# A third K panel combined in ten of the eleven up-projection groups, with raw blocks and scratch rows in four fixed tiles and the filters in two buffers

## The chip, the cores and the metric

The kernel runs on one core of one Trainium2 chip. The metric is the device time of one execution in microseconds, as the median of several runs. Before the change it is 1975.53 us (three runs, 1974.62 to 1976.78).

## The reference

One layer of a hybrid streaming encoder runs over two request groups that share the weights: a prompt of 256 rows and eight samples of 16 rows, 384 rows in all. The change lies in the last part, the feed-forward network. DM is 2048 and D_FF is 5632, all in float32:

```
h2 = rmsnorm(x, norm_ffn_g)
up = h2 @ w_up                              # (rows, 2048) @ (2048, 11264)
g_half = up[..., :D_FF]
u_half = up[..., D_FF:]
ext_f = jnp.concatenate([ffn_buf.astype(g_half.dtype), g_half], axis=1)
gc = causal_dwconv(ext_f, ffn_dw_w, ffn_dw_b)   # 3 taps along the rows, a filter per column
x = x + (jax.nn.silu(gc) * u_half) @ w_down     # (rows, 5632) @ (5632, 2048)
```

The output also holds the last two rows of `ext_f` for the prompt and each sample.

## The kernel before

**Operands.** Every weight comes as blocks of 512 KB, two slabs of 128 rows by 512 columns, by one DMA of the SP queue each (`fetch`). A block of float32 is split into a high half, which ScalarE casts to fp32r (line 166, "hi"), and a low half, which VectorE subtracts (line 167, "lo"). A product of 128 rows is then three matmuls: with hi, with lo, and the row operand's own low half with hi (lines 1169 to 1171 in the up groups, 313 to 315 elsewhere). One block with the products made from it is a **step**; the steps of a group are counted from 0. The high and the low half stand in pairs of tiles, three pairs in the feed-forward part (`depth`, two and SPARE), so a step's split can run up to three steps ahead of TensorE.

**Up groups.** The up projection runs in eleven groups g = 0 to 10. A group makes 512 columns of the gate half (g) and the same 512 of the other half (u). Its 2048 rows of K are four panels of 512, each with two blocks for g and two for u. A plain panel multiplies the three row tiles (two of the prompt, one of the samples) with all four blocks: 4 steps of 18 matmuls, 72. A **combined** panel (`MIXED`, here panels 0 and 1) treats the prompt's two row halves, the two K halves and the two column sets as a 2 by 2 product of blocks, and makes it with seven products in place of eight, from sums of blocks on both sides. Its steps are, in the words of `steps`, b22, t3, t1, b11, t2 in the first part of the group and b21, t4 in the second, with 12, 12, 6, 12, 6, 12 and 6 matmuls, 66. t1 to t4 are sums of blocks, made by VectorE: t3 is b22 + b12 in a tile of its own (line 208), t1 is b12 + b11 in place (line 213), and t2 and t4 add b11 and b21 to the running sum (line 217). A combined panel takes seven splits and four sums, a plain one four splits. The row side's sums ("xm") are made once, while the output projection runs (`combined`); plain panels read the rows' own halves ("xg"). A group before has 22 steps and 276 matmuls.

**The order.** TensorE's order is written out by hand: the steps of a group one after the other. Other engines are ordered by a scheduler with priorities: a split is put 150 places ahead (SPLIT_AHEAD), an eviction in this part 250 (FFN_AHEAD). Each engine then works strictly in its order, and an instruction that waits holds back all behind it. `after(units, fn)` puts side work at a later tick; there is a tick per three products, that is per nine matmuls. The groups follow each other by

```
FFN_PLAN = [("up", 0)]
for n in range(0, 8, 2):
    FFN_PLAN += [("up", n + 1), ("up", n + 2), ("down", (n, n + 1))]
FFN_PLAN += [("up", 9), ("up", 10), ("down", (8, 9, 10))]
```

so groups 0, 1 and 2 come in a row, then a stretch of the down projection for the two oldest groups, and so on. A **first** group (3, 5, 7, 9) follows a down stretch, a **second** one (2, 4, 6, 8, 10) follows another up group. The last down stretch takes three groups.

**Raw blocks.** Blocks are loaded into a rotation of tiles: three called "raw", S0 and S1 from the start of this part, and S2 and S3. The down projection's partial sums ("part") use S2 and S3 too, so after a down stretch a group first loads eight blocks (ROOM) into the other five; a group that follows an up group may use all seven from its start. A load into a block begins when the low half (or the sum) that read it last is done.

**Behind a group.** Eight products gather in PSUM. The evictions (`p7`, `p1`, `q6` and so on, lines 1212 to 1247) build the rows of u and g with the help of two scratch rows e0 and e1, which are the third row of the tile "sums". The rows are then turned so that columns lie on partitions (`turned`: VectorE transposes blocks of 32 at line 328, GpSimd's DMA queue moves them through DRAM and back). Then comes the filter, four parts m = 0 to 3 of 128 columns: `fill` copies a part into a row with room for the two frames ahead (ScalarE's line 1118, then four small copies on GpSimd, lines 1121 to 1125), `taps` makes three taps and SiLU (one tap on ScalarE, line 1139, two on VectorE, line 1141), and `product` multiplies with u and splits the result for the down projection. The filter of group g runs within the next stretch: `fill` for all four parts at tick 9, the taps of part m at 10 + 2m, its product at 13 + 2m. Group 10 has 7 and a pace of 1. The rows stand in four tiles "extf" and four "gc".

**Down projection.** TensorE makes 128 by 512 products of the groups' rows; ScalarE copies them to "part", and GpSimd's queue adds them to y in DRAM. In the last stretch y is loaded back and the sum goes to the output.

Of the kernel before, what the change touches and what calls it, by code (L numbers as in the profile page):

```python
# [34 lines left out]
MIXED = (0, 1)  # L35
ROOM, SPARE = 8, 1
# [6 lines left out]
def hybrid_step(  # L43
# [90 lines left out]
    slots, wide = ["raw", "raw", "raw", "S0", "S1", "S2", "S3"], [False]  # L134

    def fetch(srcs, by_row=False, more=0):
        ok = ["raw"] + (["S0", "S1", "S2", "S3"][:2 + more] if wide[0] else [])
        slot = next(s for s in slots if s in ok)
        slots.remove(slot)
        slots.append(slot)  # L140
        if slot != "raw":
            raw = p_sg.tile([P, 2, 512], F32, tag=slot, name="raw")
        else:
            raw = wp.tile([P, 2, 512], F32, tag="raw", bufs=3, name="raw")
# [9 lines left out]
    depth = [2]  # L154
# [26 lines left out]
    PLAIN = [q for q in range(4) if q not in MIXED]  # L181
# [10 lines left out]
    def planned_mixed(w, c1, c2, first, room):  # L192
        held, count = {}, [0]

        def load(rows):
            count[0] += 1
            return fetch([rows], more=2 if count[0] > room else 0)[0]
# [25 lines left out]
        for what, q in steps(first):  # L223
# [27 lines left out]
    for what, g in FFN_PLAN:  # L251
        if what == "up":
            planned_mixed(w_up, 512 * g, DFF + 512 * g, g == 0, ROOM if g % 2 or g == 0 else 0)
# [36 lines left out]
    def gemm(jobs, sides=()):  # L290
        for js in jobs:
# [4 lines left out]
            for j, k in [(j, k + i) for k in range(0, js[0]["nk"], 2) for j in js for i in range(2)]:  # L296
# [19 lines left out]
                if sp:  # L316
                    with tc.high_priority(offset=FFN_AHEAD if wide[0] else EVAC_AHEAD):
# [634 lines left out]
    def pw_job(g):  # L952
# [8 lines left out]
        def done():  # L961
# [10 lines left out]
            for m in range(4):  # L972
# [13 lines left out]
    xg = {q: p_x2.tile([P, 2, 4, NT], F32R, name=f"xg{q}") for q in range(4) if q not in MIXED}  # L986
    xm = {q: [(gp.tile([P, 10, 2, P], F32R, tag="G4", name="xm") if (q, i) == (MIXED[-1], 0) else
               p_x2.tile([P, 10, 2, P], F32R, name=f"xm{q}{i}"))[:] for i in range(2)] for q in MIXED}
# [20 lines left out]
    def combined(n, d):  # L1009
# [27 lines left out]
        after(5, add_up)  # L1037
        after(6, halves)
        after(7, plain)

    def wo_job(n):
# [11 lines left out]
        def done():  # L1053
            d = box[0].moved()

            def parts(m):
# [3 lines left out]
                if n not in MIXED:  # L1060
# [5 lines left out]
            if n in MIXED:  # L1066
# [27 lines left out]
    extf = [p_f.tile([P, 24, 18], F32, name=f"extf{m}")[:] for m in range(4)]  # L1094
    for m in range(4):
# [4 lines left out]
    wide[0] = True  # L1100
# [6 lines left out]
    def up_g_done(g, rows, gd):  # L1107
        def done():
# [5 lines left out]
            def fill():  # L1114
                for m in range(4):
                    c = 4 * g + m
                    e = extf[m]
                    nc.scalar.copy(e[:, :, 2:18].rearrange("p (a h) x -> p a h x", h=2),
                                   gd[:, :, m, :].rearrange("p a (h x) -> p a h x", h=2))
                    e5 = e.rearrange("p (i t h) x -> p i t h x", t=NTT, h=2)  # L1120
# [218 lines left out]
```

## Time and profile before

| | before |
|---|---|
| median of three runs | 1975.53 us |
| the profiled execution | 1974.45 us |
| its span | 1972.7 us |
| clock granted to TensorE | 1.00 |
| weight loads of w_up, w_in, w_down at 512 KB | 176, 96, 88 |
| turns through DRAM: out, in (median to landing) | 120 of 192 KB (4.5 us), 30 of 768 KB (5.8 us) |
| partial sums added to y in DRAM | 16 of 768 KB (6.8 us) |

The profiled execution is one run, recorded by the hardware; its own time is 1974.45 us, of which the records span 1972.7. The feed-forward part starts at 912.6 us: groups 0 to 2 last 193.2 us, each down stretch of two groups 65.3, each pair of up groups 125.6 to 126.3, and the last down stretch 97.9.

How to read the lines that follow. The head of the page gives for each engine its busy time, its share of the span and its number of instructions (PE is TensorE's matmuls, PEld its weight loads, DVE is VectorE, ACT ScalarE, POOL GpSimd, SP SyncE, which issues the weight loads). The view by stretches gives each engine's busy time in a window. The time line has a row for each instruction: start, duration, engine, line, operation, what is written and read, the shape, and in brackets how long the engine stood idle before it and what ended that. Matmuls overlap in the pipe, so their price is the distance between two starts. The view of waits gives an engine's idle time by what it was waiting for: us, times, longest. The chain is the work that ended last in a window, each row released by the one above it. A GEMM part that waits for nothing is full at TensorE's own pace; each wait of TensorE is lost time.

### The profile page before, as it was taken

The numbers are of one execution on the slowest core, as the hardware profiler recorded it, in microseconds if no ns is written. First come the engines' busy times: TensorE is split into PE (matmuls) and PEld (weight loads), VectorE is DVE, ScalarE is ACT, GpSimd is POOL, SyncE is SP. The second block draws the span as 40 slices with busy tenths as digits, with TensorE's granted clock in tenths as the row PEclk, the third lists the DMA queues.
The fourth block names the chain that finished last, engine by engine and source line by source line (L and its number), as shares of the span: only waits on it lengthen the run. The fifth ranks groups of instructions, "written<-read, shape, count | busy, mean of one in ns | idle before, by whom it ended". The sixth has DMA issues, their size and how long they took to land. (4 is left out here: it accounts for less than half of the span.)

```text
span 1972.7 us, 24795 instructions
## 1 busy us (share of the span) xinstructions
PE 1958.7 (99%) x9254; PEld 1648.7 (84%) x9254; DVE 1265.2 (64%) x1681; ACT 887.9 (45%) x1297; POOL 254.8 (13%) x527
## 2 busy tenths in 40 slices
PE   9999999999999999999999999999999999999999
PEld 9999878888888888887887888888888888888887
DVE  4478889747465447466787647855775577557853
ACT  5433353555324423345465444553454445444541
POOL 1001121100000002111122200220022012201210
PEclk9999999999999999999999999999999999999999
DMA  6565776665344438767665576567556755666653
GB/s 185 155 173 156 229 240 201 204 183 158 113 129 128 128 128 273 234 207 228 196 186 187 172 202 182 158 188 200 162 187 180 198 178 174 194 173 193 202 188 110
DMA packets 194899, 358.20 MB, mean 182 GB/s; under 512 B 16386, under 2 KB 66557, under 8 KB 194771
## 3 DMA queue, kind: packets, MB, share of 16 engines
q1 hardware_dynamic: 172779, 272.78, 44.5%
q0 software_dynamic: 21680, 83.70, 15.4%
q8 instruction: 72, 1.18, 0.2%
q14 instruction: 48, 0.39, 0.1%
q10 hardware_dynamic: 320, 0.14, 0.0%
HBM read 301.78 MB, written 55.24 MB: 181 GB/s over the span
## 5 line engine op out<-in xcount | busy, mean ns | idle before, releaser
L167 DVE TENSOR_TENSOR lo<-raw,hi 128x1024 fp32r<-128x1024 f32 (+2 forms) x481 | 578.4, 1203 | 519.3 <-ACT hi L166 517.6
L166 ACT CAST hi<-raw 128x1024 fp32r<-128x1024 f32 (+2 forms) x481 | 497.8, 1036 | 798.1 <-PE acc L315 468.4
L313 PE MATMUL acc<-hi,hT 128*128 128x512 f32 (+1 forms) x704 | 270.4, 384 | 0.1
L314 PE MATMUL acc<-lo,hT 128*128 128x512 f32 (+1 forms) x704 | 265.7, 377 | 1.3 <-DVE lo L167 1.3
L315 PE MATMUL acc<-hi,hT 128*128 128x512 f32 (+1 forms) x704 | 265.6, 377 | 0.0
L313 PE MATMUL acc<-hi,act 128*128 128x512 f32 x484 | 188.3, 389 | 0.0
L314 PE MATMUL acc<-lo,act 128*128 128x512 f32 x484 | 188.3, 389 | 0.0
L315 PE MATMUL acc<-hi,act 128*128 128x512 f32 x484 | 188.3, 389 | 0.0
L1170 PE MATMUL acc<-lo,xg 128*128 128x512 f32 x440 | 171.7, 390 | 2.8 <-DVE lo L167 2.8
L1171 PE MATMUL acc<-hi,xg 128*128 128x512 f32 x440 | 171.4, 389 | 0.4 <-DVE xg L1063 0.4
L1169 PE MATMUL acc<-hi,xg 128*128 128x512 f32 x440 | 171.2, 389 | 0.0
L314 PEld LDWEIGHTS acc<-lo,hT 128*128 128x128 f32 x704 | 132.3, 188 | 24.5 <-DVE lo L167 3.2
L579 DVE SCALAR_TENSOR_TENSOR ut<-ext,cw,ut 128x384 f32<-128x384 f32 x240 | 149.2, 622 | 5.5
L313 PEld LDWEIGHTS acc<-hi,hT 128*128 128x128 f32 x704 | 132.2, 188 | 24.0 <-issue 1.8
L315 PEld LDWEIGHTS acc<-hi,hT 128*128 128x128 f32 x704 | 132.2, 188 | 22.7
L333 POOL DMA_DIRECT2D turn<-block x124 | 69.0, 563 | 429.3 <-DVE block L328 422.5
L1170 PE MATMUL acc<-lo,xm 128*128 128x512 f32 x308 | 120.0, 389 | 0.2 <-DVE lo L167 0.2
L1169 PE MATMUL acc<-hi,xm 128*128 128x512 f32 x308 | 119.9, 389 | 0.0
L1171 PE MATMUL acc<-hi,xm 128*128 128x512 f32 x308 | 119.8, 389 | 0.0
L314 PEld LDWEIGHTS acc<-lo,act 128*128 128x128 f32 x484 | 90.9, 188 | 18.9
L313 PEld LDWEIGHTS acc<-hi,act 128*128 128x128 f32 x484 | 90.9, 188 | 18.8
L315 PEld LDWEIGHTS acc<-hi,act 128*128 128x128 f32 x484 | 90.9, 188 | 18.8
(349 smaller groups left out, 3404.6 us busy)
## 6 DMA issues: line engine op xcount, KB each, us to landing
raw<-in_w_up_dram SPq DMA_DIRECT2D x176, 512.0 KB
raw<-in_w_in_dram SPq DMA_DIRECT2D x96, 512.0 KB
raw<-in_w_down_dram SPq DMA_DIRECT2D x88, 512.0 KB
turn<-block POOLq DMA_DIRECT2D x120, 192.0 KB, 4.5
block<-turn POOLq DMA_DIRECT2D x30, 768.0 KB, 5.8
raw<-in_w_in_dram SPq DMA_DIRECT2D x64, 256.0 KB
raw<-in_w_out_dram SPq DMA_DIRECT2D x32, 512.0 KB
y_rows<-part POOLq DMA_DIRECT2D x16, 768.0 KB, 6.8
```

The source lines that it names most:

```text
L166: nc.scalar.copy(hi[:, k, :o], raw[:, k, :o])
L167: tt(lo[:, k, :o], raw[:, k, :o], f(hi[:, k, :o]), op=ALU.subtract)
L313: mm(o, ah[:, s], hi[:, kk, :n], start=st, stop=False)
L314: mm(o, ah[:, s], lo[:, kk, :n], start=False, stop=False)
L315: mm(o, al[:, s], hi[:, kk, :n], start=False, stop=sp)
L333: nc.gpsimd.dma_start(d[:, :, i, :].rearrange("j r n -> r j n"), src[32 * i:32 * i + 32, :].rearrange("r (j n) -> r j n", j=4))
L579: stt(o, v, wc, o, op0=ALU.mult, op1=ALU.add)
L1169: mm(o, ah, hi[:, kk, :], start=st, stop=False)
L1170: mm(o, ah, lo[:, kk, :], start=False, stop=False)
L1171: mm(o, al, hi[:, kk, :], start=False, stop=last[b] == (i, n))
```

## The change

Panel 2 (`BOTH`) joins the combined panels in groups 1 to 10 (`TRIPLE`, `mixed_of`); group 0 keeps two. Such a group has 25 steps and 270 matmuls, in this order: b22, t3, t1, a plain u block, b11, t2 of panel 0; b22, t3, t1, b11, t2 of panel 1; the same five of panel 2; a plain u block, a plain g block; b21 and t4 of panels 0, 1 and 2; a plain g block. Panel 2's running sum takes the third row of "sums".

To make room, four tiles "rest" of three rows are allotted once. Their first two rows are raw blocks, so that the rotation has seven blocks at all times (no ROOM); the third rows of two of them are e0 and e1, of the other two the filter's "gc". "part" stands in two scratch blocks that the turns use too. There are two "extf" and two "gc" in place of four: `fill` goes part by part, at tick 8 + 2m, the taps at 9 + 2m, the product at 11 + 2m (group 10: 7 + m, 8 + m, 9 + m). The row side's sums for panel 2 are made at ticks 10 and 11 of the output projection; its plain forms are read from xg2, so "xm" has five entries there. In the last down stretch y takes the four "rest" tiles, and its third and fourth quarters are loaded 14 ticks later than the first two.

```diff
-MIXED = (0, 1)
-ROOM, SPARE = 8, 1
+BOTH = 2
+TRIPLE = (1, 2, 3, 4, 5, 6, 7, 8, 9, 10)
+SPARE = 1
+def mixed_of(g):
+    return (0, 1, BOTH) if g in TRIPLE else (0, 1)
...
-    slots, wide = ["raw", "raw", "raw", "S0", "S1", "S2", "S3"], [False]
-    def fetch(srcs, by_row=False, more=0):
-        ok = ["raw"] + (["S0", "S1", "S2", "S3"][:2 + more] if wide[0] else [])
-        slot = next(s for s in slots if s in ok)
-        slots.remove(slot)
+    slots = [None] * 3
+    def fetch(srcs, by_row=False):
+        slot = slots.pop(0)
         slots.append(slot)
...
+        raw = wp.tile([P, 2, 512], F32, tag="raw", bufs=3, name="raw") if slot is None else slot
...
-    def steps(first):
-        pu, pg = ([(f"p{side}{h}", q) for q in PLAIN for h in range(2)] for side in "ug")
+    def steps(g):
+        mixed = mixed_of(g)
+        pu, pg = ([(f"p{side}{h}", q) for q in range(4) if q not in mixed for h in range(2)] for side in "ug")
+        n = len(pu) // 2 if g else 0
         top, low = [], pg[:1]
-        for q in MIXED:
-            top += [(what, q) for what in ("b22", "t3", "t1")] + ([] if first else [pu.pop(0)])
+        for i, q in enumerate(mixed):
+            top += [(what, q) for what in ("b22", "t3", "t1")] + pu[i:min(i + 1, n)]
             top += [(what, q) for what in ("b11", "t2")]
-            low += [("b21", q), ("t4", q)] + pg[len(low) // 3 + 1:len(low) // 3 + 2]
-        return top + pu + low + pg[len(MIXED) + 1:]
+            low += [("b21", q), ("t4", q)] + (pg[i + 1:i + 2] if len(mixed) == 2 else [])
+        return top + pu[n:] + low + pg[len(mixed) + 1 if len(mixed) == 2 else 1:]
...
-        after(5, add_up)
-        after(6, halves)
-        after(7, plain)
+        later_by = 5 if n == BOTH else 0
+        after(5 + later_by, add_up)
+        after(6 + later_by, halves)
+        if n not in xg:
+            after(7, plain)
...
-    extf = [p_f.tile([P, 24, 18], F32, name=f"extf{m}")[:] for m in range(4)]
+    extf = [p_f.tile([P, 24, 18], F32, name=f"extf{m}")[:] for m in range(2)]
...
+    rest = panels("rest")
+    slots.extend(r[:, 0:2, :] for r in rest)
...
-    e0, e1 = plain_sums[:, 2, 0], plain_sums[:, 2, 1]
-    new_sum.append(lambda q: plain_sums[:, MIXED.index(q)])
+    e0, e1 = rest[0][:, 2, :], rest[1][:, 2, :]
+    gcs = [r[:, 2, 0:NT] for r in rest[2:]]
+    new_sum.append(lambda q: plain_sums[:, q])
...
-            lag, pace = (7, 1) if g == 10 else (9, 2)
-            after(lag, fill)
+            lag, pace = (7, 1) if g == 10 else (8, 2)
...
             for m in range(4):
+                after(lag + pace * m, lambda m=m: fill(m))
                 after(lag + 1 + pace * m, lambda m=m: taps(m))
-                after(lag + 2 + pace * m + pace, lambda m=m: product(m))
+                after(lag + 2 + pace * m + pace // 2, lambda m=m: product(m))
...
         def mixed(q, j):
-            return [(xm[q][0][:, j, i], xm[q][1][:, j, i]) for i in range(2)]
+            if j < 5 or q not in xg:
+                return [(xm[q][0][:, j, i], xm[q][1][:, j, i]) for i in range(2)]
+            t, h = ((0, 0), (0, 1), (1, 1), (2, 0), (2, 1))[j - 5]
+            return [tuple(xg[q][:, part, 2 * h + i, t * P:(t + 1) * P] for part in range(2)) for i in range(2)]
...
-                    box.append(p_sg.tile([P, NTT * 512], F32, tag=f"S{2 + n % 2}", name="part"))
+                    box.append(block(2 + n % 2))
...
-            y[:] = panels("y")
+            del slots[3:]
+            slots[:] = [None] * 3
+            y[:] = rest
+            def reload(n):
+                nc.gpsimd.dma_start(y[n][:].rearrange("p t n -> p (t n)"), y_rows[n][:])
             for n in range(4):
-                nc.gpsimd.dma_start(y[n][:].rearrange("p t n -> p (t n)"), y_rows[n][:])
+                after(14 if n > 1 else 0, lambda n=n: reload(n))
```

Lines of the kernel after are up to eight higher: 166 is 167, 167 is 168, 208 is 209, 213 is 214, 217 is 218, 328 is 329, and 1118, 1139, 1141 are 1123, 1142, 1144.

Two places show how the order of the engines moves. The first is VectorE's at the start of group 6, a second group, before the change: the last eviction of group 5 (line 1247), the transposes of its gate rows ("block", line 328) and the low halves of group 6's steps 2 to 7 ("lo" and "lo3", line 167). "raw" is a loaded block, "sums" a running sum, and the brackets name whose semaphores an instruction waits for (DMAHW is a load).

```order
L1247 SCALAR_TENSOR_TENSOR block_11341<-acc_11307,r2_6760,sums_7732 128x512 [waits PE_49]
L328 STREAM_TRANSPOSE block_11456<-block_11341 128x4x4x32 [waits DMASW5_49,DMASW4_49,DMASW6_49,DMASW3_49,DVE_49]
L167 TENSOR_TENSOR lo_11479<-raw_11428,hi_11478 128x1024 [waits PE_49,Activation_49]
L328 STREAM_TRANSPOSE block_11456<-block_11341 128x4x4x32 [waits DVE_49]
L328 STREAM_TRANSPOSE block_11456<-block_11341 128x4x4x32
L167 TENSOR_TENSOR lo3_6749<-raw_11496,hi3_6748 128x1024 [waits DMAHW4_49,Activation_49]
L167 TENSOR_TENSOR lo_11514<-raw_11475,hi_11513 128x1024 [waits Activation_49]
L167 TENSOR_TENSOR lo_11526<-sums_7732,hi_11525 128x1024 [waits Activation_49]
L167 TENSOR_TENSOR lo3_6749<-raw_11548,hi3_6748 128x1024 [waits Activation_49]
L167 TENSOR_TENSOR lo_11570<-sums_7732,hi_11569 128x1024 [waits Activation_49]
```

The same place after the change, from the low half of step 2 to that of step 7, with "rest" for raw blocks in the four fixed tiles:

```order
L168 TENSOR_TENSOR lo_11432<-raw_11386,hi_11431 128x1024 [waits PE_49,Activation_49]
L329 STREAM_TRANSPOSE block_11414<-block_11319 128x4x4x32 [waits DMASW5_49,DMASW4_49,DMASW6_49,DMASW3_49,DVE_49]
L329 STREAM_TRANSPOSE block_11414<-block_11319 128x4x4x32 [waits DVE_49]
L168 TENSOR_TENSOR lo3_6749<-rest1_7740,hi3_6748 128x1024 [waits DMAHW4_49,Activation_49]
L329 STREAM_TRANSPOSE block_11414<-block_11319 128x4x4x32
L209 TENSOR_TENSOR sums_7738<-raw_11588,raw_11613 128x1024 [waits DMAHW1_49,DMAHW0_49]
L168 TENSOR_TENSOR lo_11466<-rest0_7739,hi_11465 128x1024 [waits Activation_49]
L168 TENSOR_TENSOR lo_11478<-sums_7738,hi_11477 128x1024 [waits Activation_49]
L168 TENSOR_TENSOR lo3_6749<-rest2_7741,hi3_6748 128x1024 [waits Activation_49]
L214 TENSOR_TENSOR raw_11613<-raw_11613,rest0_7739 128x1024 [waits DMAHW3_49,DVE_49]
L168 TENSOR_TENSOR lo_11520<-sums_7738,hi_11519 128x1024 [waits Activation_49]
```

The sum t3 of panel 2 (line 209), which waits for two loads, now stands ahead of the low half of step 4, and the sum t1 of panel 2 (line 214), which waits for another, ahead of that of step 7, where before the low halves followed each other with one load waited for.

The second place is ScalarE's in the middle of group 6, where the filter of group 5 runs (fills into "extf", first taps into "gc", and high halves "hi" between them), before the change:

```order
L1118 COPY extf0_7724<-block_11457 128x24x16 [waits DMASW7_49]
L1118 COPY extf1_7725<-block_11457 128x24x16
L166 CAST hi_11636<-raw_11580 128x1024 [waits DMAHW7_49,DVE_49,PE_49]
L1118 COPY extf2_7726<-block_11457 128x24x16
L166 CAST hi_11647<-sums_7732 128x1024 [waits DVE_49,PE_49]
L1118 COPY extf3_7727<-block_11457 128x24x16
L1139 ACTIVATE gc_11470<-extf0_7724,col_202,fw_208 128x384 [waits Activation_49,Pool_49]
L1139 ACTIVATE gc_11471<-extf1_7725,col_202,fw_208 128x384 [waits Activation_49,Pool_49]
L1139 ACTIVATE gc_11472<-extf2_7726,col_202,fw_208 128x384 [waits Activation_49,Pool_49]
L1139 ACTIVATE gc_11473<-extf3_7727,col_202,fw_208 128x384 [waits Activation_49,Pool_49]
L166 CAST hi3_6748<-raw_11673 128x1024 [waits DMAHW1_49,DVE_49,PE_49]
```

And after it, down to the high halves of steps 12 and 13, where "rest2" and "rest3" stand for the third rows that hold the filter:

```order
L167 CAST hi_11573<-sums_7738 128x1024 [waits DVE_49,PE_49,Activation_49]
L1123 COPY extf0_7734<-block_11415 128x24x16 [waits DMASW7_49]
L167 CAST hi_11590<-raw_11588 128x1024 [waits DMAHW0_49,DVE_49,PE_49]
L1142 ACTIVATE rest2_7741<-extf0_7734,col_202,fw_208 128x384 [waits Activation_49,Pool_49]
L1123 COPY extf1_7735<-block_11415 128x24x16
L1142 ACTIVATE rest3_7742<-extf1_7735,col_202,fw_208 128x384 [waits Activation_49,Pool_49]
L167 CAST hi3_6748<-sums_7738 128x1024 [waits DVE_49,PE_49]
L167 CAST hi_11631<-raw_11613 128x1024 [waits DVE_49,PE_49]
```

Before, four fills come ahead of four taps; now a fill, a high half and a tap alternate, and each of the two taps waits for GpSimd's copies ("Pool") with the high half of a step right behind it.

More of the change, by code (lines that the diff above doesn't have):

```diff
@@ L180, in hybrid_step, with planned_mixed @@
     sums, new_sum = {}, []
-    PLAIN = [q for q in range(4) if q not in MIXED]
-    def steps(first):
-        pu, pg = ([(f"p{side}{h}", q) for q in PLAIN for h in range(2)] for side in "ug")
+    def steps(g):
+        mixed = mixed_of(g)
+        pu, pg = ([(f"p{side}{h}", q) for q in range(4) if q not in mixed for h in range(2)] for side in "ug")
+        n = len(pu) // 2 if g else 0
         top, low = [], pg[:1]
-        for q in MIXED:
-            top += [(what, q) for what in ("b22", "t3", "t1")] + ([] if first else [pu.pop(0)])
+        for i, q in enumerate(mixed):
+            top += [(what, q) for what in ("b22", "t3", "t1")] + pu[i:min(i + 1, n)]
             top += [(what, q) for what in ("b11", "t2")]
-            low += [("b21", q), ("t4", q)] + pg[len(low) // 3 + 1:len(low) // 3 + 2]
-        return top + pu + low + pg[len(MIXED) + 1:]
-    def planned_mixed(w, c1, c2, first, room):
-        held, count = {}, [0]
+            low += [("b21", q), ("t4", q)] + (pg[i + 1:i + 2] if len(mixed) == 2 else [])
+        return top + pu[n:] + low + pg[len(mixed) + 1 if len(mixed) == 2 else 1:]
+    def planned_mixed(w, c1, c2, g):
+        held = {}
         def load(rows):
-            count[0] += 1
-            return fetch([rows], more=2 if count[0] > room else 0)[0]
+            return fetch([rows])[0]
         def add(fn):
@@ L222, in planned_mixed @@
                 "b21": lambda q: single("b21", 4 * q + 2, c1), "t4": lambda q: grown(q, "b21")}
-        for what, q in steps(first):
+        for what, q in steps(g):
             if what[0] == "p":
@@ L316, in gemm @@
                 if sp:
-                    with tc.high_priority(offset=FFN_AHEAD if wide[0] else EVAC_AHEAD):
+                    with tc.high_priority(offset=FFN_AHEAD if ffn[0] else EVAC_AHEAD):
                         for m in range(nb):
@@ L985, in hybrid_step @@
     spare = [[p_x2.tile([P, 2, 512], F32R, name=f"{n}{i}")[:] for n in ("hi", "lo")] for i in range(3, 3 + SPARE)]
-    xg = {q: p_x2.tile([P, 2, 4, NT], F32R, name=f"xg{q}") for q in range(4) if q not in MIXED}
-    xm = {q: [(gp.tile([P, 10, 2, P], F32R, tag="G4", name="xm") if (q, i) == (MIXED[-1], 0) else
-               p_x2.tile([P, 10, 2, P], F32R, name=f"xm{q}{i}"))[:] for i in range(2)] for q in MIXED}
+    xg = {BOTH: p_x2.tile([P, 2, 4, NT], F32R, name=f"xg{BOTH}"), 3: gp.tile([P, 2, 4, NT], F32R, tag="G4", name="xg3")}
+    xm = {q: [p_x2.tile([P, 5 if q == BOTH else 10, 2, P], F32R, name=f"xm{q}{i}")[:] for i in range(2)]
+          for q in (0, 1, BOTH)}
     p_w, close_w = pool("norm2", side="right")
@@ L1059, in parts @@
                 nc.scalar.activation(v, v, AF.Identity, scale=g)
-                if n not in MIXED:
+                if n in xg:
                     hi, lo = natural(xg[n][:, 0, m, :]), natural(xg[n][:, 1, m, :])
@@ L1092, in hybrid_step @@
     after(8, lambda: nc.scalar.copy(sft[:], sin.rearrange("p (a c) -> p a c", c=32)[:, :, 0:16]))
-    extf = [p_f.tile([P, 24, 18], F32, name=f"extf{m}")[:] for m in range(4)]
-    for m in range(4):
+    extf = [p_f.tile([P, 24, 18], F32, name=f"extf{m}")[:] for m in range(2)]
+    for m in range(2):
         nc.gpsimd.memset(extf[m][:, 0, 0:2], 0.0)
@@ L1133, in taps @@
                 c = 4 * g + m
[L1134 removed]
+                a = gcs[m % 2]
+                o = a.rearrange("p (a t) -> p a t", t=16)
                 for w in range(3):
[L1136 removed]
+                    v = extf[m % 2][:, :, w:w + 16]
                     wc = fw[:, w * 44 + c:w * 44 + c + 1]
@@ L1252, in up_group @@
         seq = [plain(q, int(what[2]), *({"u": ("q3", "q2", "tu"), "g": ("p2", "q4", "tg")}[what[1]]))
-               if what[0] == "p" else pairs(q, *made[what]) for what, q in steps(g == 0)]
+               if what[0] == "p" else pairs(q, *made[what]) for what, q in steps(g)]
         run(seq, forms, dict(p5=None, p7=out(p7), q3=out(q3), tu=sample("u"), q2=out(q2), p1=out(p1), q6=out(q6),
```

43 lines of the change are left out of this document (17 added, 26 removed).

## Prediction

> **What bounds the kernel now.** I read the head of the page first, then the busy time by stretches, then TensorE's own waits and its time line, and last the chain of waits where a group begins.
>
> ```profile
> span 1972.7 us, 24795 instructions
> PE 1958.7 (99%) x9254; PEld 1648.7 (84%) x9254; DVE 1265.2 (64%) x1681; ACT 887.9 (45%) x1297; POOL 254.8 (13%) x527
> ```
>
> TensorE is busy for 99% of the span, so its matmuls are the bound, as long as their operands come in time. The next view gives three stretches: the first up group of a pair (group 3), the second (group 4), and the down projection behind it.
>
> ```profile
> core 0: us, PE busy (x) PEld busy (x) DVE busy (x) ACT busy (x) POOL busy (x), PEclk, DMA share, GB/s
> 1171.05:1233.90 62.85, 62.48 (x276) 51.44 (x275) 43.90 (x42) 27.05 (x29) 3.67 (x6) 1.00 0.63 180
> 1233.90:1296.80 62.90, 62.90 (x279) 52.12 (x278) 48.29 (x58) 33.85 (x44) 13.13 (x29) 1.00 0.54 169
> 1296.80:1362.10 65.30, 65.30 (x289) 54.08 (x289) 33.68 (x40) 30.70 (x44) 12.06 (x27) 1.00 0.70 197
> ```
>
> The clock is 1.00 throughout. VectorE works 48.3 of 62.9 us in the second group, since the filter of the group before stands there, and only 33.7 of 65.3 us in the down projection. So VectorE's room lies in the down stretches, and this change adds its work to the up stretches.
>
> ```profile
> PE acc L1170 <- DVE lo L167: 3.1, 5, 1.4
> PE misc L1170 <- DVE lo L167: 1.2, 4, 0.4
> ```
>
> TensorE's waits from 905 us on: nine, 4.3 us in all, every one for a low half. The price of a matmul is the distance between starts, not its length of 0.39 us:
>
> ```profile
> 959.70 0.39 PE L1169 MATMUL acc<-hi,xm 128*128 128x512 f32 x1
> ...
> 981.69 0.39 PE L1170 MATMUL acc<-lo,xm 128*128 128x512 f32 x1
> ```
>
> These are the first and the 98th row of an unbroken run: 21.99 us over 97 distances, 0.2267 us each. A group of 276 then takes 62.57 us, and the two groups above took 62.85 and 62.90: about 0.3 us each is waiting. Where the waiting comes from is shown by the chain at the start of group 5:
>
> ```profile
> 1362.06 0.24 PE acc L315
> ...
> 1362.80 1.06 ACT hi L166
> ...
> 1363.88 1.24 DVE lo L167
> ...
> 1365.14 6.04 DMA raw<-in_w_up_dram
> ...
> 1371.27 1.23 DVE raw L213
> 1372.49 1.15 DVE lo L167
> ```
>
> The low half of step 2 (steps are counted from 0) frees a raw block, the load into that block takes 6.04 us, and a sum that needs the load stands on VectorE ahead of the low half of step 4. That half is out at 1373.6, 11.5 us after the group's start; TensorE wanted it after 48 matmuls, 10.9 us. VectorE works in order, so a sum that waits for its load holds back every low half behind it.
>
> **The change, part by part.** *Matmuls.* In ten groups the third panel costs 66 instead of 72, which the order of TensorE confirms (60 rows fewer): 60 x 0.2267 = 13.6 us less. It falls on the bound.
>
> *VectorE's added work.* Per group three more splits and four more sums of 128x1024, and in pace:
>
> ```profile
> 1256.01 1.23 DVE L167 TENSOR_TENSOR lo<-raw,hi 128x1024 fp32r<-128x1024 f32 x1 [0.62 <-ACT hi L166]
> ...
> 1261.77 1.23 DVE L217 TENSOR_TENSOR sums<-sums,raw 128x1024 f32<-128x1024 f32 x1 [1.03 <-DMA raw<-in_w_up_dram]
> 1262.91 1.22 DVE L167 TENSOR_TENSOR lo<-raw,hi 128x1024 fp32r<-128x1024 f32 x1
> 1264.05 0.55 DVE L1147 TENSOR_TENSOR gc<-block,gc 128x384 f32<-128x384 f32 x1
> ```
>
> Back to back they start 1.14 us apart, so 7 x 1.14 = 8.0 us per group. A second group then asks 48.3 + 8.0 = 56.3 us of VectorE in 270 x 0.2267 = 61.2 us: 92%. It still fits, so the sum of work alone costs nothing; what it loses is room for waits. A first group asks 51.9 of 61.2. ScalarE's three more high halves (1.06 each) bring it to 37 of 61.2.
>
> *The order of loads and sums: the term I rest on.* With three panels combined, panel 2's first sum stands between the low halves of steps 3 and 4, its second ahead of step 7, and the running sum of panel 0 ahead of step 11 (order, second group). By the rotation of seven blocks these loads go into the blocks freed by the low halves of steps 2, 4 and 8. Let x be the time from such a low half to the landing. Rows show x = 6.0 (chain above) and x = 4.5: the low half begun at 1256.01 ended at 1257.24, and the sum waiting for its load started at 1261.77.
>
> ```profile
> 1234.58 0.74 DVE L1244 SCALAR_TENSOR_TENSOR block<-acc,r,block 128x512 f32<-128x512 f32 x1
> 1235.24 0.74 DVE L1247 SCALAR_TENSOR_TENSOR block<-acc,r,sums 128x512 f32<-128x512 f32 x1
> 1235.90 0.70 DVE L328 STREAM_TRANSPOSE block<-block 128x512 f32<-128x512 f32 x1
> ```
>
> A second group begins with two evictions of 0.66 (starts above), a sum and the low half of step 2: 0.2 + 2 x 0.66 + 2 x 1.14 = 3.8, with a semaphore 3.9 us. The low half of step 4 is then out at 3.9 + x + 2.4 (sum 1.14, low half 1.23); TensorE wants it at 48 matmuls plus one, since the low half enters with the second: 11.1. Step 7: x + 2.4 later; wanted after 79 matmuls, 17.9. Step 8's half is 2.3 behind that, step 11's x + 2.4 behind that; wanted after 115, 26.1. Lateness moves the later wants along.
> With x = 4.5: 10.8 (in time), 17.7 (in time), 26.9 (0.8 late).
> With x = 6.0: 12.3 (1.2 late), 20.7 (1.6 more), 31.4 (2.5 more): 5.3 us.
> I take 5.0 for the first two, which run beside the transfers that turn the last gate rows, and 4.5 for the third: 11.3 (0.2), 18.7 (0.6), 27.9 (1.0), together 1.8 us, rounded up to 1.9 for the restart of the matmul pipe. Six groups have this form (1, 2, 4, 6, 8, 10): 6 x 1.9 = 11.4 us. The bounds are nothing (the four deeper blocks hide the loads) and 6 x 5.3 = 31.8. First groups keep the one late step that they have.
>
> [...]
>
> *Filters in two buffers.* Fills come one by one, and ScalarE's first tap waits for GpSimd between fill and tap, twice, before the high half of step 12 (order). Three of GpSimd's four copies of one filter take:
>
> ```profile
> 1254.75 0.70 POOL L1123 COPY extf<-extf 128x16 f32<-128x16 f32 x1 [7.74 <-ACT extf L1118]
> 1255.38 0.20 POOL L1124 COPY extf<-extf 128x12 f32<-128x12 f32 x1
> 1255.52 0.18 POOL L1125 COPY extf<-extf 128x2 f32<-128x2 f32 x1
> ...
> 1257.88 0.81 POOL L1123 COPY extf<-extf 128x16 f32<-128x16 f32 x1 [0.33 <-ACT extf L1118]
> 1258.63 0.59 POOL L1124 COPY extf<-extf 128x12 f32<-128x12 f32 x1
> 1259.16 0.57 POOL L1125 COPY extf<-extf 128x2 f32<-128x2 f32 x1
> ```
>
> Start to end 0.95 or 1.85 us. ScalarE's own part, two taps and a fill, is 2 x 0.6 + 0.4 = 1.6 us:
>
> ```profile
> 1257.24 0.51 ACT L1118 COPY extf<-block 128x384 f32<-128x384 f32 x1
> 1257.65 1.91 ACT L1139 ACTIVATE gc<-extf,col,fw 128x384 f32<-128x384 f32 x3
> ```
>
> Twice GpSimd's part and that is 3.5 to 5.3 us; from the end of step 8 to step 12 TensorE takes 30 matmuls, 6.8 us, less 2.3 for both halves of step 12: 4.5. So from 1.0 early to 0.8 late; I take nothing, because step 11 is late already and moves the want along.
>
> The Trainium skill, "GPSIMD Engine Reference" (Specifications), says that GpSimd shares its SBUF interfaces with VectorE and contends with VectorE instructions of two SBUF inputs, of which this change adds 70. The trace agrees (0.95 against 1.85 us for the same copies); by the free price the term is nothing, by the contended one up to 6 x 0.8 = 4.8.
>
> *Group 2's extra operands* are made while the output projection runs:
>
> ```profile
> 880.00:912.60 32.60, 32.60 (x145) 27.00 (x144) 18.66 (x22) 15.15 (x24) 4.64 (x7) 1.00 0.73 235
> ...
> L1030 DVE TENSOR_TENSOR xm<-block,xm 128x1280 fp32r<-128x1280 f32 x2 | 3.0, 1492 | 0.0
> ...
> L1023 DVE TENSOR_TENSOR block<-block 128x256 f32<-128x256 f32 x2 | 0.8, 419 | 0.0
> ```
>
> 5 x 0.42 + 1.49 = 3.6 us of VectorE, beside 18.7 in its last 32.6 us: hidden, and first read a group later. Down sums move to two scratch rows whose next writer comes some 40 us later; the reload of y moves within the last down projection. Both nothing; without that cover, one transfer of y, about 6 us.
>
> *Sum:* -13.6 + 11.4 = -2.2. The profiled execution took 1974.45 us (span 1972.7), 1.1 below the median of 1975.53; 1974.45 - 2.2 + 1.1 = **1973.3 us**.
>
> **Rivals.** *The gain stays.* Seven blocks are there from the start of every group, where now a first group begins with five, and the loads land in 4.5 us or less: 6 x 0.8 = 4.8 us given back, -8.8, 1966.7. For it: the 4.5 us row and VectorE's 8% of room. Against it: three links follow each other with hardly a plain step between. [...]
> *The chain locks up.* With x = 5.5 the three are late by 0.7, 1.1 and 2.0, 3.8 a group, 22.8 in all: +9.2, 1984.7. It decides from about x = 5.25, where six groups give back 18 us. For it: the 6.04 row. Against it: that load runs beside the down projection's last transfers.
> *The filters bind.* GpSimd's copies at the contended price hold ScalarE before step 12 on top of the forecast, 4.8 us, and the same again at the third and fourth filter: +7.4, 1982.9. The page on GpSimd above names the mechanism.
> That the change does not do what it says is excluded by the order of TensorE.
>
> **How the numbers follow.** Forecast 0.38, the gain stays 0.36, the chain locks up 0.19, the filters bind 0.07. A measurement of this kernel tells about 0.2% (4 us) from no change, so these are also the chances: faster 0.36, same 0.38, slower 0.26. The range reaches from 1964 (the bound of nothing given back is 1975.5 - 13.6 = 1961.9) to 1988 (x = 5.7); the bound of x = 6.0, 1993.7, is left out, as is the last piece of the other. The forecast's own range is 1971.5 to 1979.5.
>
> **What would show it.** Right: TensorE's waits for the low half rise from 4.3 us to some 15, at steps 4, 7 and 11 of second groups, each behind a sum that waits for its load; first groups last 61.5 us, second ones 63. If second groups last under 62, the gain has stayed; over 65, the chain has locked up. If step 12 is late behind ScalarE's tap on GpSimd, the filters bind. Wrong altogether: a wait in the down stretches, or behind scratch rows.

## The result, and the profile after

The changed kernel takes **1988.94 us** (median of six runs, 1983.62 to 1990.33) where the kernel before takes 1976.55 (six runs, 1974.62 to 1977.22): 1.0063 times as long, with a 95% interval of 1.0052 to 1.0073. The forecast was 1973.3 and the range 1964 to 1988. The profiled execution took 1983.62 us, the fastest of the six, with a span of 1981.9: 9.2 us longer than before's.

The head of the page, and the view by stretches for the same three places as before (group 3, group 4, the down projection behind them; busy us and, in brackets, instructions of each engine, then clock, share of the DMA engines and GB/s):

```profile
span 1981.9 us, 24797 instructions
PE 1951.8 (98%) x9194; PEld 1635.5 (83%) x9194; DVE 1345.2 (68%) x1757; ACT 919.2 (46%) x1328; POOL 271.6 (14%) x525
```

```profile
1172.80:1237.30 64.50, 62.12 (x271) 50.43 (x270) 47.40 (x45) 30.07 (x32) 3.67 (x6) 1.00 0.56 160
1237.30:1301.20 63.90, 62.10 (x271) 50.38 (x271) 57.05 (x66) 36.81 (x47) 15.45 (x28) 1.00 0.57 174
1301.20:1366.50 65.30, 65.30 (x290) 54.06 (x289) 35.25 (x41) 30.80 (x44) 13.56 (x28) 1.00 0.70 204
```

The 60 matmuls are gone, and TensorE is busy for only 7 us less, in a span 9 us longer. The down stretch is as it was. Both up groups are longer than before (62.85 and 62.90), although they hold six matmuls fewer. (From first matmul to first matmul they last 64.55 and 63.87 us, before 63.23 and 62.56: the stretch of group 3 before ends 0.38 us early. Group 3 waited 0.67 us then and group 4 not at all, where the prediction read about 0.3 us in each. Its nine waits, all for low halves, leave out a tenth, 0.4 us for a row operand in group 0.) TensorE's waits from 905 us on (engine, tile and line of the matmul, what it waited for, us, times, longest):

```profile
PE acc L1174 <- DVE lo L168: 10.2, 13, 1.7
PE acc L1173 <- DVE block L1230: 5.8, 5, 1.3
PE acc L1173 <- ACT xg L1065: 2.9, 1, 2.9
PE misc L1174 <- DVE lo L168: 1.7, 5, 0.5
PE acc L1173 <- ACT hi L167: 0.2, 1, 0.2
```

Low halves (lines 1174) rose from 4.3 to 11.9 us, as the forecast had it in kind. The second row is new: a first matmul of a product (line 1173, with hi, not lo) waits for an **eviction** by VectorE (line 1230), so for a PSUM bank. The third is group 0's first plain block of panel 3, which waits for a row operand that ScalarE writes ("xg").

To see where each wait stands, the starts of all matmuls are laid against the steps. What a step loses is the sum of its distances above 0.2267 us, all in us over the ten groups 1 to 10, with group 0 apart, and distances of about twice that, matmuls at half the clock (last section), apart. The third column is a later profile of the same kernel:

| lost | before | after | the same kernel once more |
|---|---|---|---|
| group 0 | 3.56 | 4.21 | 4.46 |
| steps 2 to 11 | 3.15 | 13.06 | 13.37 |
| step 12 | 1.59 | 5.35 | 5.99 |
| steps 16 and 17 | 0.0 | 9.59 | 8.80 |
| matmuls at half the clock | 0.0 | 0.19 | 4.41 |
| first up group starts at | 912.61 | 911.37 | 913.25 |

After against before: 0.65 + 9.91 + 3.76 + 9.59 + 0.19 lost more, 1.24 for the earlier start and 13.60 for the matmuls gained: +9.3 us; the two executions differ by 9.2. (The 0.19 is a single distance of 0.416 us; the clock is 1.00 throughout that profile.) Three places have to be explained: steps 2 to 11, step 12, and steps 16 and 17.

**Step 17** is the first plain g block. Its fourth matmul is the first of q4's product and opens the bank for it. The time line of VectorE and of TensorE in group 4:

```profile
1277.04 0.68 DVE L1225 TENSOR_TENSOR rest<-misc,rest 128x512 f32<-128x512 f32 x1
1277.64 1.21 DVE L168 TENSOR_TENSOR lo<-raw,hi 128x1024 fp32r<-128x1024 f32 x1
1278.77 0.74 DVE L1226 SCALAR_TENSOR_TENSOR rest<-rest,nr,rest 128x512 f32<-128x512 f32 x1
1279.43 0.55 DVE L1154 TENSOR_TENSOR act<-rest,act 128x384 fp32r<-128x384 f32 x1
1279.90 0.74 DVE L1229 SCALAR_TENSOR_TENSOR block<-acc,nr,rest 128x512 f32<-128x512 f32 x1
1280.56 0.74 DVE L1230 SCALAR_TENSOR_TENSOR block<-acc,nr,block 128x512 f32<-128x512 f32 x1
```

```profile
1281.35 0.50 PE L1173 MATMUL acc<-hi,xg 128*128 128x512 f32 x1 [1.33 <-DVE block L1230]
```

Product q6 is complete with step 15. Its eviction is four instructions of VectorE (1225, 1226, 1229, 1230) with one of ScalarE between them, and only the last gives back the bank of p5, which is the one that q4 is to take. Between step 15 and step 17 there is now one plain u block, 18 x 0.2267 = 4.1 us. Before there were two, 8.2 us, since both plain u blocks that were left stood behind the last t2. The four evictions with a low half and a product of the filter between them end at 1281.3; step 15 had ended near 1275.1 (1281.35 less 1.5 of waiting and 21 matmuls), and a sum and a low half stood ahead of the first.

**Step 6** loses 1.9 to 2.1 us in groups 1, 3 and 9. The chain of waits at the start of group 3 (start, us, what; each row released by the one above):

```profile
1174.56 1.24 DVE lo L168
...
1175.81 6.26 DMA raw<-in_w_up_dram
...
1182.17 1.23 DVE sums L209
1183.40 1.15 DVE lo L168
...
1184.56 3.67 DMA raw<-in_w_up_dram
...
1188.32 1.22 DVE raw L214
1189.54 1.15 DVE lo L168
...
1190.73 0.50 PE acc L1174
```

Two loads in series. The first goes into the block freed by the low half of step 2. The sum that needs it holds back the low half of step 4, which frees the block of the second load, and the sum that needs that one holds back step 6. In groups 5 and 7 the second load takes a block freed by step 3, starts without waiting for the first sum, and step 6 loses nothing.

**Step 12** in groups 4, 6, 8 and 10, here in group 4:

```profile
1261.97 0.41 POOL extf L1128
1262.38 1.13 POOL extf L1129
1263.51 0.53 POOL extf L1130
...
1264.68 1.05 ACT hi L167
...
1265.75 2.36 DVE lo L168 x2
```

and on ScalarE's time line the tap (line 1142) with the high half behind it:

```profile
1264.07 0.71 ACT L1142 ACTIVATE rest<-extf,col,fw 128x384 f32<-128x384 f32 x1 [2.22 <-POOL extf L1130]
1264.68 1.04 ACT L167 CAST hi<-sums 128x1024 fp32r<-128x1024 f32 x1
```

The high half of step 12 stands behind a tap that waits for GpSimd's copies of the second filter part, 2.1 us for three of them.

### The profile page after: what moved, and what is told of

The parts are those of the page before. It is cut to its first block, busy times and chain, and to the rows that moved or that the text cites. A ratio compares the mean times of both kernels' runs of the same rounds, so it can differ in the third digit from the quotient of the medians.

```text
span 1981.9 us, 24797 instructions
## 1 busy us (share of the span) xinstructions
PE 1951.8 (98%) x9194; PEld 1635.5 (83%) x9194; DVE 1345.2 (68%) x1757; ACT 919.2 (46%) x1328; POOL 271.6 (14%) x525
## 4 chain that ended last, share of the span: by engine, by line
PE 77%; DVE 11%; DMA 6%; issue 3%; ACT 2%; POOL 1%; DVEq 0%; SPq 0%; ACTq 0%; POOLq 0%
PE acc L314 16%; PE acc L315 16%; PE acc L316 16%; DVE lo L168 5%; PE acc L1174 4%; PE acc L1173 4%; PE acc L1175 4%; PE acc L311 2%; DMA raw<-in_w_up_dram 2%; PE acc L309 2%; PE acc L310 2%; PE misc L1174 2%; DMA rest<-in_w_up_dram 2%; PE misc L1175 2%; PE misc L1173 2%
## 5 line engine op out<-in xcount | busy, mean ns | idle before, releaser
L168 DVE TENSOR_TENSOR lo<-raw,hi 128x1024 fp32r<-128x1024 f32 (+2 forms) x345 | 412.7, 1197 | 357.5 <-ACT hi L167 356.9
L167 ACT CAST hi<-raw 128x1024 fp32r<-128x1024 f32 (+2 forms) x345 | 354.8, 1029 | 599.8 <-PE acc L316 417.2
L167 ACT CAST hi<-rest 128x1024 fp32r<-128x1024 f32 x136 | 142.5, 1049 | 150.0 <-PE acc L1175 66.3
L168 DVE TENSOR_TENSOR lo<-rest,hi 128x1024 fp32r<-128x1024 f32 x136 | 165.5, 1219 | 63.8 <-ACT hi L167 62.9
L1174 PE MATMUL acc<-lo,xm 128*128 128x512 f32 x388 | 152.7, 394 | 9.6 <-DVE lo L168 9.5
L1173 PE MATMUL acc<-hi,xm 128*128 128x512 f32 x388 | 151.3, 390 | 0.2 <-ACT hi L167 0.2
L1175 PE MATMUL acc<-hi,xm 128*128 128x512 f32 x388 | 151.2, 390 | 0.0
L316 PEld LDWEIGHTS acc<-hi,hT 128*128 128x128 f32 x704 | 132.1, 188 | 22.8
L167 ACT CAST hi<-sums 128x1024 fp32r<-128x1024 f32 x96 | 101.0, 1052 | 102.7 <-PE acc L1175 53.1
L168 DVE TENSOR_TENSOR lo<-sums,hi 128x1024 fp32r<-128x1024 f32 x96 | 116.5, 1214 | 28.1 <-ACT hi L167 27.8
L1173 PE MATMUL acc<-hi,xg 128*128 128x512 f32 x300 | 118.0, 393 | 9.3 <-DVE block L1230 5.8
L1174 PE MATMUL acc<-lo,xg 128*128 128x512 f32 x300 | 117.1, 390 | 0.7 <-DVE lo L168 0.7
```

The costliest lines, as they stand in the source:

```text
L167: nc.scalar.copy(hi[:, k, :o], raw[:, k, :o])
L168: tt(lo[:, k, :o], raw[:, k, :o], f(hi[:, k, :o]), op=ALU.subtract)
L316: mm(o, al[:, s], hi[:, kk, :n], start=False, stop=sp)
L1173: mm(o, ah, hi[:, kk, :], start=st, stop=False)
L1174: mm(o, ah, lo[:, kk, :], start=False, stop=False)
L1175: mm(o, al, hi[:, kk, :], start=False, stop=last[b] == (i, n))
```

## The experiments

Each kernel was timed against the kernel before on the same chip, and ratios are to that. All change the changed kernel.

**The rest of the change alone.**

```diff
-TRIPLE = (1, 2, 3, 4, 5, 6, 7, 8, 9, 10)
+TRIPLE = ()
```

> The changed kernel with no third panel combined in any group (two panels in every group, 22 steps, 276 matmuls); fixed blocks, scratch rows, two filter buffers and all else of the change stay. Theory: the loss comes from the third panel's steps, since the wait of step 17 for a PSUM bank (8.0 us in the profile) and the double chain of loads before step 6 need it; so this kernel takes the time of before, 1974 to 1979 us. Rival: the narrower filter and the fixed blocks cost something by themselves; then 1981 us or more, with waits of TensorE for high halves behind ScalarE's taps.

Measured: 1974.22 us, 0.9992 (0.9983 to 1.0001). From group 4 to group 9 each group lasts 62.56 us, which is 276 x 0.2267: no wait is left there, not even the late step 4 of first groups. Its waits of TensorE from 905 us on:

```profile
PE acc L1173 <- ACT xg L1065: 2.7, 1, 2.7
PE acc L1174 <- DVE lo L168: 1.0, 2, 0.7
```

Fixed blocks, scratch rows and two filter buffers cost nothing by themselves that the interval would show. The whole loss comes with the third panel.

**The bank.** In the first plain g block q4's matmuls come last:

```diff
+        def by_bank(prods):
+            return [p for b in ("p2", "tg", "q4") for p in prods if p[0] == b]
...
-        seq = [plain(q, int(what[2]), *({"u": ("q3", "q2", "tu"), "g": ("p2", "q4", "tg")}[what[1]]))
+        seq = [(by_bank if g in TRIPLE and what == "pg0" else list)(plain(q, int(what[2]), *names(what)))
```

> The changed kernel, with the 18 matmuls of the first plain g block in another order: p2, then the samples' product, then q4, so that q4's bank is asked for 9 matmuls (2.04 us) later. Theory: the wait of step 17 is for the bank of p5, which VectorE gives back 1.5 us late in second groups and 0.3 in first ones; it goes, and 7 to 8 us with it: about 1981 us against 1989. Rival: VectorE is the bound there (56 of 61 us), and the wait comes back in the next steps as late low halves: less than 3 us gained.

Measured: 1983.77 us, 1.0041 (1.0028 to 1.0053), 5.5 us under the changed kernel on this chip, less than the 7 to 8 expected. Steps 16 and 17 lose 0.8 us in place of 8.8, so the wait was for the bank, and the row for the eviction is gone from TensorE's waits:

```profile
PE acc L1174 <- DVE lo L168: 9.3, 12, 1.8
PE misc L1174 <- DVE lo L168: 3.8, 5, 2.2
PE acc L1173 <- ACT xg L1065: 2.6, 1, 2.6
PE acc L1173 <- ACT hi L167: 1.0, 1, 1.0
```

Steps 2 to 11 lose 16.6 in place of 13.4: some of the gain came back as low halves.

**The order of the sums.** Every sum stays behind the low half two steps before its own, by a dependency without a semaphore:

```diff
+    def in_order(d):
+        tc.add_manual_dep(d.ins, los[-2], mybir.DependencyInfo(
+            mybir.DependencyClass.NoSync, mybir.DependencyReason.DATA), reason="sums")
...
-            tt(sums[q], held["b22"][:], single("b12", 4 * q, c2)[:], op=ALU.add)
+            in_order(tt(sums[q], held["b22"][:], single("b12", 4 * q, c2)[:], op=ALU.add))
```

(and so for the other two; `los` lists the low halves by name)

> The changed kernel with every sum of an up group held on VectorE until the low half two steps before its own step is issued, so that no sum that waits for its load stands ahead of earlier low halves. Theory: the waits of steps 3, 4, 6, 7 and 11 (some 10.5 us in the profile) are low halves behind such sums; they go, 8 to 10 us: about 1980 us. Rival: the loads themselves come too late for their steps; then low halves and sums wait for them at steps 6 to 13 in place of these, and less than 3 us is gained.

Measured: 1982.12 us, 1.0027 (1.0017 to 1.0037), 7.2 under the changed kernel. Steps 2 to 11 lose 0.6 us in place of 13.4. The loads are in time for their own steps; only the place of the sums made low halves late. Step 12 loses 0.7 in place of 6.0, and nothing in groups 4, 6, 8 and 10: the scheduler put the second tap earlier here, 22.1 us into group 4 and not 26.7. Its waits:

```profile
PE acc L1177 <- DVE block L1234: 12.7, 11, 2.4
PE acc L318 <- ACT act L1157: 3.8, 1, 3.8
PE acc L1178 <- DVE lo L168: 3.0, 6, 0.6
```

(1177 and 1234 are 1173 and 1230 with four lines added.) Now that TensorE is no longer held ahead of step 17, the bank is waited for eleven times, once of them in group 0: steps 16 and 17 of groups 1 to 10 lose 13.3. Step 23 loses 3.6 to low halves. A new wait stands in the last down stretch (line 318).

**The changed kernel once more.**

> The changed kernel itself, once more, as the measure for the others on this chip and for a second profile. Theory: about 1989 us, and the 5 us by which most of its runs exceed the profiled one come from the chain of loads before step 6, which in the profile is late by 1.8 us in groups 1, 3 and 9 and not in 5 and 7. Rival: they come from elsewhere, a clock under 1.00 or the stages before the up groups.

Measured: 1989.31 us, 1.0068 (1.0055 to 1.0080), profiled at 1990.17. Its column stands in the table above: the waits of each row are the same within 1 us, groups 5 and 7 again lose nothing at step 6. Of the 6.5 us more than in the first profile, 4.2 are matmuls at half the clock and 1.9 the later start of the up groups. So the theory fell, and the rival was right.

**Taps one tick later**, alone and with both edits:

```diff
-                after(lag + 1 + pace * m, lambda m=m: taps(m))
+                after(lag + pace + pace * m, lambda m=m: taps(m))
```

> The changed kernel with the taps of each filter one tick (2 us) later in groups 0 to 9, so that ScalarE's tap waits for GpSimd's copies behind the high half of step 12 and not ahead of it. Theory: the waits of step 12 in groups 4, 6, 8 and 10 (0.6 to 2.2 us each in the two profiles, 3.4 and 4.2 us in all) go: 3 to 4 us faster than the changed kernel, about 1985.5. Rival: VectorE's two taps then fall beside the evictions that free the bank for step 17, and that wait grows by as much: no gain, or slower.

> All three edits: q4 last, sums in order, taps one tick later. Theory: the high half of step 12 no longer stands behind a tap, another 3 us under the run with two edits: 1964 to 1970. Rival: as for the taps alone, the filter moves into the evictions of q6, and it is as slow as two edits or slower.

Measured: 1987.89 us alone, 1.0056 (1.0043 to 1.0070), and 1972.45 with both edits, 0.9982 (0.9973 to 0.9990): nothing gained in either. Both differences lie within the intervals. The traces show why this tells nothing: the scheduler left the tap ahead of the high half of step 12 all the same, and the step loses 0.8 us in groups 4, 6 and 8 as before. The ninth run puts the tap behind it.

**Both edits.**

> The two edits of the second and third run together: q4's matmuls last in the first plain g block, and sums held in the order of their steps. Theory: the two kinds of waits are separate, and each edit alone left the other's (13 us of low halves with the first, 12.7 us of the bank with the second); together they give back more than the 5.5 and 7.2 us that they gave alone, 16 to 22 us under the changed kernel: 1967 to 1973, so below the kernel before. Rival: both draw on VectorE's last 5 us of each second group, and together they give less than the sum: above 1977.

Measured: 1972.56 us, 0.9980 (0.9971 to 0.9989), the first kernel faster than before by more than its interval. By the ratios that is some 17 us under the changed kernel, more than the 12.7 of the two edits alone. Groups 3, 5, 7 and 9 last 61.20 us, which is 270 x 0.2267, and no step in 2 to 11 loses anything; step 12 still loses 3.7. What is left:

```profile
PE acc L1178 <- DVE lo L168: 3.6, 7, 1.1
PE acc L318 <- ACT act L1157: 3.4, 1, 3.4
PE acc L318 <- DVE block L1255: 2.6, 1, 2.6
PE acc L1177 <- DVE block L1234: 2.4, 1, 2.4
```

Two waits of the down projection (line 318): the first down stretch lasts 69.82 us and the last 101.79, where they had 65.28 and 97.92. These are the two that follow groups 2 and 10.

**Eight groups.** Both edits, `TRIPLE = (1, 3, 4, 5, 6, 7, 8, 9)`, and `by_bank` for the first plain g block of every group.

> The two edits (q4 last, here in every group's first plain g block, and sums in order) with the third panel combined in groups 1 and 3 to 9 only; groups 2 and 10 keep two panels. Theory: with two edits the up groups were clean, and what was lost stood in the first and in the last down stretch (69.8 and 101.8 us instead of 65.3 and 97.9), where the filters of groups 2 and 10 come too late behind a VectorE that is full in these groups; both losses (8.4 us) and the slow start of group 0's first g block (2.5 and 1.6 us) go, and 2 x 0.5 us of gain with them: 1961 to 1965. Rival: the lateness comes from the filter's new places and buffers, and these two stretches stay as long: 1972 or more.

Measured: **1959.94 us**, 0.9918 (0.9904 to 0.9931). The down stretches are back at 65.28 and 97.92, group 0 lasts 63.92 in place of 67.58, and no matmul runs at half the clock. Giving up two of the ten panels, with the reordered g block of group 0, brought some 12 us: 8.4 in the two stretches, 3.7 in group 0.

**The tap behind the high half**, in the same eight groups:

```diff
+                        if m == 1 and pace == 2:
+                            tc.add_manual_dep(d.ins, his[-1], mybir.DependencyInfo(
+                                mybir.DependencyClass.NoSync, mybir.DependencyReason.DATA), reason="tap")
-                after(lag + 1 + pace * m, lambda m=m: taps(m))
+                after(lag + pace + pace * m, lambda m=m: taps(m))
```

> As the run with eight groups, and the second tap of each filter held on ScalarE until the high half of step 12 is issued, in groups 4, 6 and 8, with taps one tick later. The fifth run had meant this, but there the tap still stood ahead of the high half. Theory: the 0.62 us of TensorE at step 12 in these three groups go, 1.9 us in all, which rounds can hardly show but the trace does. Rival: step 12's low half is late for VectorE's sake, and the 0.62 us stay.

Measured: **1957.43 us**, 0.9906 (0.9892 to 0.9919). The interval overlaps that of the run before; on this chip all four executions (1956.70 to 1958.74) lie under the five of that run (1958.94 to 1960.58). ScalarE's time line in group 4 without the edit, then with it:

```profile
1253.62 0.71 ACT L1146 ACTIVATE rest<-extf,col,fw 128x384 f32<-128x384 f32 x1 [2.78 <-POOL extf L1134]
1254.24 1.03 ACT L167 CAST hi<-sums 128x1024 fp32r<-128x1024 f32 x1
```

```profile
1251.65 1.06 ACT L167 CAST hi<-sums 128x1024 fp32r<-128x1024 f32 x1 [1.02 <-PE misc L1182]
1253.41 0.71 ACT L1146 ACTIVATE rest<-extf,col,fw 128x384 f32<-128x384 f32 x1 [0.71 <-POOL extf L1134]
```

The high half ("hi<-sums") passes the tap, and step 12 loses 0.0 in place of 2.9 us over all groups (0.6 of it, in group 1, now stands at step 11); groups 4, 6 and 8 go from 62.1 to 61.20 us. Its stretches of groups 3 and 4 and the down projection:

```profile
1165.80:1227.00 61.20, 61.20 (x272) 50.67 (x271) 49.53 (x47) 29.95 (x32) 3.67 (x6) 1.00 0.59 169
1227.00:1288.20 61.20, 61.20 (x272) 50.68 (x271) 56.13 (x63) 35.89 (x45) 12.95 (x24) 1.00 0.52 169
1288.20:1353.40 65.20, 65.20 (x289) 54.01 (x288) 34.62 (x42) 31.99 (x47) 14.40 (x32) 1.00 0.77 216
```

TensorE is busy for all of them, with VectorE at 56.1 of 61.2 us.

**First groups only**, no edits: `TRIPLE = (3, 5, 7, 9)`.

> The changed kernel with the third panel combined in groups 3, 5, 7 and 9 only, the first of each pair, and none of the edits. The prediction had these groups at 61.5 us, 1.1 us under the 62.6 of two panels each; by that 1974.2 - 4.4 = 1969.8 us. Theory now: two of the four lose 1.8 us at step 6 to the chain of two loads and all lose at steps 4 and 17, so 1974 to 1977 us, no gain against two panels everywhere.

Measured: 1974.73 us, 1.0000 (0.9991 to 1.0009). The four groups last 64.23, 62.29, 62.03 and 64.12 us against 62.56 with two panels: groups 3 and 9 lose 2.0 and 1.9 at step 6. Even where VectorE has room the panel brings nothing without the edits. The order of the sums alone is not enough either: in the third run groups 3, 5, 7 and 9 last 62.6 us, and 61.20 only with both.

The kernels in one table. They ran on three chips, so the ratios are to be compared:

| kernel | us | ratio to before |
|---|---|---|
| two panels everywhere | 1974.22 | 0.9992 |
| first groups only | 1974.73 | 1.0000 |
| the changed kernel | 1989.31 | 1.0068 |
| taps later | 1987.89 | 1.0056 |
| q4 last | 1983.77 | 1.0041 |
| sums in order | 1982.12 | 1.0027 |
| both | 1972.56 | 0.9980 |
| both, taps later | 1972.45 | 0.9982 |
| both, eight groups | 1959.94 | 0.9918 |
| both, eight groups, tap behind | 1957.43 | 0.9906 |

## Why the prediction was wrong

**The step that failed** is "It still fits, so the sum of work alone costs nothing; what it loses is room for waits". The sum was right (56.3 us forecast for a second group, 57.05 measured, and the last kernel runs at 56.1 without a wait). What was left out is the room itself, as a span in which VectorE must be done with something: the change takes two plain u blocks to one between the product q6 and the first plain g block, and with them 4.1 us in which VectorE evicts q6. This wait for a bank was in no term and in no rival. It is 9.6 us in the profile and 8.8 in the second one. The second run shows that it is the bank. With the 3.8 us more at step 12, mostly the filters', which were taken at nothing too, it turns the forecast's -2.2 us into the +9.2 of the profile; loads and sums came out 1.5 under their term, and group 0 and the earlier start take 0.6 off.

**Loads and sums** were the term the forecast rested on, 11.4 us. Steps 2 to 11 lost 9.9 us more than before, and the mechanism was right: the third run takes it away by moving the sums alone. The place was wrong, and that the size came near is in part luck: the six groups of the forecast lost 5.8 us more and not 11.4, and the other 4.1 stand in first groups. The forecast had six groups that follow an up group late at steps 4, 7 and 11, and "First groups keep the one late step that they have". In the trace groups 4 and 8 lose 0.4 us or less there, and groups 3 and 9 lose 2 us at step 6, where load and sum come twice in series. Which block of the rotation a load takes decides that, and it differs from group to group. The loads' times, 6.26 and 3.67 us in that chain, lie around the 4.5 to 6.0 of the forecast.

**Filters in two buffers** were taken at nothing, with a rival of 4.8 us and as much again. The rival's mechanism was right, at the named place: steps 12 of groups 4, 6, 8 and 10 lost 0.8, 0.8, 0.8 and 1.6 us in the profile. (The 1.4 us of group 2 there is a load, 6.22 us, and not the filter.) GpSimd's copies were dearer than both prices of the forecast: 2.1 us for three in group 4, beside a sum and a low half on VectorE. Nor was 0.95 the price without VectorE: the first of those copies, 0.70 us, ran beside a low half (1254.17 to 1255.39 before), and only the other two, 0.2 us each, beside none. "Step 11 is late already and moves the want along" did not hold, since step 11 was hardly late. With the tap behind the high half the loss is gone in groups 4, 6 and 8; group 10 with three panels was not tried so.

**Scratch rows, fixed blocks, group 2's operands, the reload of y** at nothing: right within the interval of the first run.

**The matmuls**, 13.6 us: right, and with the waits removed all of them show. A group of 270 lasts 61.20 us.

**The clock** was taken as 1.00 throughout. In the second profile of the changed kernel it is not (0.997 over the execution), and the matmuls at half the clock, 4.4 us, are in no term. They and the later start of the up groups make 6.1 of the 6.5 us between the two profiles. That the same lifts the median 5 us above the first profile is likely but not shown: four of the other five executions have a clock of 0.998 or 0.999, but one of 1989.08 us has 1.000.

The rivals: the gain did not stay, and the chain did not lock up, since the links seldom followed each other. That this rival's +9.2 us is also the difference of the two profiles is chance: it had 22.8 us of late loads, and the trace has 9.9. The end on the slower side came from three mechanisms at once, of which one was not seen.

What stays open: why the first and last down stretches came late with ten groups and both edits. The last one came late with the order of the sums alone, too (the wait of 3.8 us at line 318). That both are in time without the third panel of groups 2 and 10 is shown, with group 0's g block changed in the same run; through which instruction they came late was not tried by itself. Late turns of the rows of u, behind a full VectorE, would fit the trace of the last one: the transposes of the gate rows begin 10.6 us into the stretch and the filter's first fill 29.7, where they begin 3.0 and 21.6 us into it in the changed kernel without edits.

## What to carry to other kernels

When steps with slack are traded for shorter ones, count not only the busy time of the helping engine but each span in which it must finish something: here the distance in matmuls between a product's end and the first product that needs its bank. On an engine that works in order, an instruction that waits for a load must not stand ahead of work that is ready; a dependency that fixes its place was worth 7 us alone and, with the bank's wait gone, turned a loss into a gain. And a saving should be taken only where it is free: eight groups were some 12 us faster than ten, 3.7 of it by group 0's reordered block.

## What the hardware showed that was not expected

A wait of TensorE can cost more than itself. In the second profile of the changed kernel, behind a wait of 2.4 us in group 1, matmuls start 0.43 us apart in place of 0.2267 (PE time line), and the granted clock is 0.58 over the 4.0 us from that wait's end, and 0.99 over the next 5.0. (Waits are given here as the distance between two starts less 0.2267; the bracket in a row is some 0.16 less.)

```profile
1000.63 0.50 PE L1174 MATMUL acc<-lo,xm 128*128 128x512 f32 x1 [2.25 <-DVE lo L168]
...
1001.54 0.63 PE L1174 MATMUL acc<-lo,xm 128*128 128x512 f32 x1
1001.97 0.63 PE L1175 MATMUL acc<-hi,xm 128*128 128x512 f32 x1
1002.39 0.63 PE L1173 MATMUL acc<-hi,xm 128*128 128x512 f32 x1
```

```profile
1000.60:1004.60 4.00, 3.97 (x11) 3.12 (x12) 3.47 (x3) 0.00 (x0) 0.00 (x0) 0.58 0.45 142
1004.60:1009.60 5.00, 5.00 (x23) 4.13 (x22) 3.07 (x3) 3.63 (x6) 2.48 (x6) 0.99 0.55 153
```

Such runs of 5 to 13 matmuls stand behind waits of 2.0 to 4.0 us in eight of the ten experiments' profiles, 1 to 3 times each, at some 0.2 us a matmul. They don't follow every such wait: none stands behind the 3.08 us in the first profile of the changed kernel, and behind the 3.57 us of the last down stretch one stands with all three edits and none with two. Behind single waits under 1.9 us there is none, and none in the kernels without long waits (before, and the last two of eight groups). In group 10 a run stands, in two profiles of three, behind two waits of 1.2 and 1.0 us that follow each other closely. What decides it is not shown.

The Trainium skill, "TensorE: Matmul & The Clock Gate" (Part 1: The HAM clock gate), says that the clock goes to half after an idle window of about 3.4 us which runs free of the kernel. The half clock and its dependence on chance agree with the traces. The length does not: single waits of 2.0 to 3.3 us were enough here in eight of the ten profiles, and for this kernel the measurement counts.
